# An experts' loop with a pinned order on four engines, the output product taken from two parts of both sides, and three overflow blocks moved into the loop

## The chip, the cores and the metric

The kernel runs on one core of one Trainium2 chip. Its five engines work side by side, each through its own queue of instructions in order: TensorE (PE, with its weight loads as PEld), ScalarE (ACT), VectorE (DVE), GpSimd (POOL) and SyncE (SP), which only issues DMAs here. The metric is the device time of one execution in microseconds (us), the median of three runs. Before the change it is 2878.36 us (2875.5 to 2880.1).

## The reference, cut to what matters

A trunk of two layers over 1024 tokens of 1024 features. Each layer ends in a mixture of 32 experts; every token goes to two of them. The change touches only this part:

```python
def routed_experts(ht, gate_w, expert_id, w_gate, w_up, w_down):
    ...
    def block_mlp(args):
        tok, e = args
        xb = h_pad[tok]
        hid = jax.nn.silu(xb @ w_gate[e]) * (xb @ w_up[e])
        return hid @ w_down[e]
    yb = lax.map(block_mlp, (row_tok.reshape(n_blocks, ROW_BLOCK), block_e))
    y = jax.ops.segment_sum(yb.reshape(R, D) * row_w[:, None], row_tok, num_segments=T + 1)
```

A block is 128 rows of one expert. `w_gate` and `w_up` of an expert are 1024x256 each, `w_down` is 256x1024, all float32: 3 MB for one expert.

## The kernel before, in words

The experts' stage of a layer is `moe` (L1583). Each of the 32 experts has one block of up to 128 slots, done in a loop (L1676). What does not fit goes to overflow blocks, done after the loop behind a branch on their count; with these inputs three of them run in each layer.

For one expert `e`:

- `gather` (L1594): POOL issues an indirect DMA that brings the expert's rows of the normalised input into `xg`, one of two buffers.
- `prepare` (L1606): PE turns `xg` by eight transposes into `xT_ps`; ACT copies it, rounded, to `xT_hi`, and DVE subtracts to get the rest, `xT_lo`.
- `split_half` (L1575): the gate and up weights come in two halves of 1 MB (`w_gu`, a ring of five buffers, loaded by SP). ACT casts a half to `w_hi`, DVE subtracts to get `w_lo`. There are three pairs of them.
- `up` (L1623): 24 matmuls (eight slices of the features, three products hi*hi, lo*hi and hi*lo) into `h_ps`; `hidden` (L1615) makes the activation `th` of it on ACT and DVE.
- `down` (L1645): two transposes of `th` into `hT_ps`, a copy back by DVE, then the output product `y_ps` in plain float32 with `w_d` (a ring of three buffers). DVE scales it into `yo` (one buffer), and POOL issues the indirect DMA that scatters `yo` to `yd` in HBM.

The loop's text gives `up(e)`, the splits, `gather(e + 2)`, `prepare(e + 1)`, `down(e - 1)` and the loads of later experts. The text is not the order on the engines: a scheduler with a timeline of its own decides that, by what it holds to be ready. The overflow blocks work in plain float32 throughout (`up_late`, L1638, and the same `down`).

`route_overflow` (L1490) works out the overflow blocks' tables; its instructions lie beside the first experts. After the stage, `sum_of` loads `yd` back, so the last scatter must have landed.

Of the kernel before, what the change touches and what calls it, by code (L numbers as in the profile page):

```python
# [10 lines left out]
F32 = mybir.dt.float32  # L11
F32R = mybir.dt.float32r
# [3 lines left out]
OP = mybir.AluOpType  # L16
# [4 lines left out]
T = 1024  # L21
D = 1024
NT = 8
NK = 8
# [28 lines left out]
class Trunk:  # L53
# [18 lines left out]
    GAP_A = (1.2, 0.3)  # L72

    def pool(self, **kw):
        if kw.get("space") is not DRAM:
            kw["reuse_waits"] = "tile"
        return self.tc.tile_pool(**kw)

# [1411 lines left out]
    def route_overflow(self, w, psum):  # L1490
# [20 lines left out]
        big = [w.tile([128, 1024], F32, name="ro_big", tag="ro") for _ in range(2)]  # L1511
        in1, in2 = (x[0:1, 0:480].rearrange("p (b e) -> p b e", e=32) for x in big)
# [9 lines left out]
        tmp = big[0][:, 512:1024].rearrange("p (t e) -> p t e", e=32)  # L1522
# [16 lines left out]
        o1 = big[0][:, 512:768].rearrange("p (t b) -> p t b", b=16)  # L1539
        nc.vector.tensor_tensor(o1, io[:, None, 0:16].to_broadcast([128, 16, 16]), bf.to_broadcast([128, 16, 16]), op=OP.is_equal)  # L1540
        oc = big[1][:, 512:1024].rearrange("p (t j b) -> p t j b", j=2, b=16)
# [15 lines left out]

    def more_tiles(self, wp):
        self.parts = [[wp.tile([128, 4, 512], F32R, name=f"w_{n}{i}") for n in ("lo", "hi")] for i in (2, 1, 0)][::-1]
        self.raw += [wp.tile([128, 4, 512], F32, name=f"w_gu{i}") for i in range(2, 5)]  # L1560
# [6 lines left out]
    def load_gu(self, l, i, e):  # L1567

        for half in range(2):
            self.nc.sync.dma_start(self.raw[(2 * i + half) % 5], self.expert_source(l, e, "moe_w_gu")[half])  # L1570

    def load_d(self, l, i, e):
        self.nc.sync.dma_start(self.wd[i % 3], self.expert_source(l, e, "moe_w_down"))

    def split_half(self, n, eng=None):  # L1575

        nc = self.nc
        raw = self.raw[n % 5]
        lo, hi = self.parts[n % 3]
        nc.scalar.copy(hi, raw)  # L1580
        (eng or nc.vector).tensor_tensor(lo, raw, hi.bitcast(F32), op=OP.subtract)  # L1581

    def moe(self, l, side, psum):  # L1583

        nc, tc = self.nc, self.tc
        with ExitStack() as s:
# [3 lines left out]
            for x in xg:  # L1590
                nc.gpsimd.memset(x, 0.0)
            scat = []
# [22 lines left out]
            def hidden(ph):  # L1615
                x = tx.tile([128, 512], F32, name="th", tag="mt")
                th = x[:, 0:256]
# [3 lines left out]
                return x  # L1621

            def up(e, x):  # L1623
                hi, lo = x
                ph = psum.tile([128, 512], F32, name="h_ps", tag="h", bufs=2)
                for k in range(NK):
                    wlo, whi = self.parts[(2 * e + k // 4) % 3]
# [3 lines left out]
                return hidden(ph)  # L1631

            def prepare_late(e):
                pt = transposed(e)
                nc.scalar.copy(late[e % 2], pt)
                return late[e % 2]

            def up_late(e, x):  # L1638

                ph = psum.tile([128, 512], F32, name="h_ps", tag="h", bufs=2)  # L1640
                for k in range(NK):
                    nc.tensor.matmul(ph, x[:, k, :], self.raw[(2 * e + k // 4) % 5][:, k % 4, :], start=(k == 0), stop=(k == NK - 1))
                return hidden(ph)

            def down(e, th):  # L1645
                w = self.wd[e % 3]
                pt = psum.tile([128, 2, 128], F32, name="hT_ps", tag="hT", bufs=1)
                for k in range(2):
                    nc.tensor.transpose(pt[:, k, :], th[:, 128 * k:128 * k + 128], self.ident)  # L1649
                hT = th[:, 256:512].rearrange("p (a b) -> p a b", a=2)  # L1650
                nc.vector.tensor_copy(hT, pt)  # L1651
                po = psum.tile([128, D], F32, name="y_ps", tag="y", bufs=1)
# [4 lines left out]
                yo = tx.tile([128, D], F32, name="yo", tag="x", bufs=1)  # L1657
                nc.vector.scalar_tensor_tensor(yo, po, self.wsl[:, e:e + 1], gt2, op0=OP.mult, op1=OP.mult)  # L1658
                st = nc.gpsimd.indirect_dma_start(out=self.yd, out_offset=bass.IndirectOffsetOnAxis(ap=self.idx_s[:, e:e + 1], axis=0),  # L1659
                                                  in_=yo, in_offset=None, bounds_check=2 * T - 1, oob_is_err=False)  # L1660
                for o in scat:
                    tc.declare_no_dep(st.ins, o.ins, reason="every slot holds another row")
                scat.append(st)
# [4 lines left out]
            def overflow(b):  # L1668
                eb = block_weights(b)
                self.load_gu(l, 32 + b, eb)  # L1670
                self.load_d(l, 32 + b, eb)

            gather(0)
            gather(1)
            x, prev = prepare(0), None
            for e in range(32):  # L1676
                th = up(e, x)
                for n in (2 * e + 3, 2 * e + 4):
                    if n < 64:
                        self.split_half(n)  # L1680
                if e + 1 < 32:
                    if e + 2 < 32:
                        gather(e + 2)
                    x = prepare(e + 1)
                if e == 0:
                    nc.sync.dma_start(gt2, self.mod_row(l, 5).partition_broadcast(128))
                if prev is not None:
                    down(*prev)
                prev = (e, th)
                if e < 28:  # L1690
                    self.load_gu(l, e + 4, e + 4)
                if 0 < e < 30:
                    self.load_d(l, e + 2, e + 2)
                if e == 2:
                    self.route_overflow(xp, psum)
                if e == 29:
                    self.load_gu(l, 32, block_weights(0))
            late = [xp.tile([128, 8, 128], F32, name="xT", tag="ro") for _ in range(2)]
            gather(32)
            gather(33)  # L1700
            self.load_d(l, 32, block_weights(0))
            down(*prev)
            x = prepare_late(32)

            n = nc.values_load(self.ovf[0:1, 0:1], min_val=0, max_val=15)
            with ExitStack() as ifs:
                for b in range(15):
                    ifs.enter_context(tc.If(n > b))
                    if b + 2 < 15:
                        gather(34 + b)  # L1710
                    if b + 1 < 15:
                        overflow(b + 1)
                    down(32 + b, up_late(32 + b, x))
                    if b + 1 < 15:
                        x = prepare_late(33 + b)
# [38 lines left out]
    def layer(self, l, x_src):  # L1754

        nc = self.nc
# [12 lines left out]
        def more():  # L1769

            self.wo_stack.close()
            self.more_tiles(se.enter_context(self.pool(name=f"wE{l}", bufs=1, side=here)))
            self.load_gu(l, 1, 1)
            for n in range(3):
                self.split_half(n, nc.gpsimd)
            for e in (2, 3):
                self.load_gu(l, e, e)

        with ExitStack() as s:
            psum = Banks(**{n: s.enter_context(self.pool(name=f"ps{n}e{l}", bufs=b, space=PSUM))  # L1780
                            for n, b in (("tp", 2), ("po", 4), ("pl", 2))})
            self.out_proj(l, there, psum, lambda: (self.load_gu(l, 0, 0), self.load_d(l, 0, 0)), more)
        if l == 0:
            self.dump("xm", self.xm)
        with ExitStack() as s:
            psum = s.enter_context(self.pool(name=f"psE{l}", bufs=1, space=PSUM))
            wp = s.enter_context(self.pool(name=f"wD{l}", bufs=1, side=here))
            self.wd += [wp.tile([128, 2, D], F32, name=f"w_d{i}") for i in range(1, 3)]
            for e in (1, 2):
                self.load_d(l, e, e)  # L1790
            self.moe(l, there, psum)
# [114 lines left out]
```

## Time and profile before

| what | us |
|---|---|
| median of three runs | 2878.36 |
| profiled execution | 2890.55 |
| its span, first to last instruction | 2888.7 |
| PE busy | 2452.3 (85%) |
| DVE busy | 1845.5 (64%) |
| ACT busy | 1063.5 (37%) |
| POOL busy | 721.3 (25%) |

The span is what the trace covers; the profiled execution is some 2 us longer than its span and 12 us longer than the median. The two experts' stages lie at about 1031 to 1448 us and 2424 to 2836 us of the span. Busy shares are averages over stages that have different limits, so the stage has to be read by itself.

### The profile page before, as it was taken

The numbers are of one execution on the slowest core, as the hardware profiler recorded it, in microseconds if no ns is written. First come the engines' busy times: TensorE is split into PE (matmuls) and PEld (weight loads), VectorE is DVE, ScalarE is ACT, GpSimd is POOL, SyncE is SP. The second block draws the span as 40 slices with busy tenths as digits, with TensorE's granted clock in tenths as the row PEclk, the third lists the DMA queues.
The fourth block names the chain that finished last, engine by engine and source line by source line (L and its number), as shares of the span: only waits on it lengthen the run. The fifth ranks groups of instructions, "written<-read, shape, count | busy, mean of one in ns | idle before, by whom it ended". The sixth has DMA issues, their size and how long they took to land.

```text
span 2888.7 us, 45371 instructions
## 1 busy us (share of the span) xinstructions
PE 2452.3 (85%) x17281; PEld 1842.3 (64%) x17281; DVE 1845.5 (64%) x3927; ACT 1063.5 (37%) x1908; POOL 721.3 (25%) x569
## 2 busy tenths in 40 slices
PE   5999987998789779999849888889877986999991
PEld 3766666787678656666427666778756775666650
DVE  5358785555684767767264689756467566776745
ACT  3333332343463224444133343334345331444421
POOL 4122232222420511111141222221242032111113
PEclk8989998998899779999969989899889986999996
DMA  8477575452442359899551434453443224998874
GB/s 285 157 233 215 178 239 135 134 147 93 161 127 93 140 190 328 312 329 336 188 203 52 136 122 140 151 155 115 127 158 114 98 100 147 342 350 317 306 261 186
DMA packets 264230, 548.99 MB, mean 190 GB/s; under 512 B 77048, under 2 KB 181440, under 8 KB 233280
## 3 DMA queue, kind: packets, MB, share of 16 engines
q1 hardware_dynamic: 235424, 490.90, 50.6%
q0 software_dynamic: 23952, 40.99, 3.9%
q10 hardware_dynamic: 4624, 14.06, 1.2%
q8 instruction: 141, 2.31, 0.3%
q14 instruction: 89, 0.73, 0.1%
HBM read 467.68 MB, written 120.09 MB: 203 GB/s over the span
## 4 chain that ended last, share of the span: by engine, by line
PE 52%; DVE 23%; DMA 11%; ACT 7%; issue 5%; POOL 1%; SPq 1%; DVEq 0%; ACTq 0%; POOLq 0%
PE y_ps L1655 8%; PE pj L335 5%; PE pj L336 5%; PE pj L337 5%; DVE w_lo L1581 4%; ACT w_hi L1580 4%; PE h_ps L1629 3%; PE h_ps L1628 2%; DVE sv_m L724 2%; DVE sv_t L726 2%; PE h_ps L1630 2%; PE po L1284 2%; DMA ada_w<-in_ada_w 2%; DMA yd<-yo,idx_s 2%; PE po L1285 2%
## 5 line engine op out<-in xcount | busy, mean ns | idle before, releaser
L1581 DVE TENSOR_TENSOR w_lo<-w_gu,w_hi 128x2048 fp32r<-128x2048 f32 x122 | 279.6, 2292 | 206.3 <-ACT w_hi L1580 202.1
L1580 ACT CAST w_hi<-w_gu 128x2048 fp32r<-128x2048 f32 x128 | 244.0, 1908 | 384.6 <-PE h_ps L1629 367.4
L335 PE MATMUL pj<-hh,wa_hi 128*128 128x512 f32 x800 | 341.6, 427 | 2.7 <-ACT wa_hi L322 1.9
L336 PE MATMUL pj<-hl,wa_hi 128*128 128x512 f32 x800 | 332.0, 415 | 1.1 <-DVE hl L312 1.1
L337 PE MATMUL pj<-hh,wa_lo 128*128 128x512 f32 x800 | 328.9, 413 | 3.3 <-POOL wa_lo L323 3.3
L1655 PE MATMUL y_ps<-w_d,th 128*128 128x512 f32 x560 | 260.3, 608 | 40.9 <-DVE th L1651 25.5
L1628 PE MATMUL h_ps<-w_hi,xT_hi 128*128 128x512 f32 x512 | 225.8, 441 | 3.9 <-ACT xT_hi L1611 3.9
L1629 PE MATMUL h_ps<-w_hi,xT_lo 128*128 128x512 f32 x512 | 210.8, 412 | 2.6 <-DVE xT_lo L1612 2.6
L1630 PE MATMUL h_ps<-w_lo,xT_hi 128*128 128x512 f32 x512 | 203.2, 397 | 0.0
L1655 PEld LDWEIGHTS y_ps<-w_d,th 128*128 128x128 f32 x560 | 101.3, 190 | 156.9 <-issue 103.3
L323 POOL TENSOR_TENSOR wa_lo<-wa_raw,wa_hi 128x1024 fp32r<-128x1024 f32 x50 | 122.0, 2441 | 315.6 <-ACT wa_hi L322 262.0
L335 PEld LDWEIGHTS pj<-hh,wa_hi 128*128 128x128 f32 x800 | 157.8, 197 | 42.0 <-issue 7.4
L337 PEld LDWEIGHTS pj<-hh,wa_lo 128*128 128x128 f32 x800 | 156.8, 196 | 39.5 <-POOL wa_lo L323 4.6
L336 PEld LDWEIGHTS pj<-hl,wa_hi 128*128 128x128 f32 x800 | 157.8, 197 | 37.2 <-issue 4.5
L1659 POOL DMA_INDIRECT yd<-yo,idx_s x70 | 70.5, 1008 | 402.2 <-DVE yo L1658 323.6
L1595 POOL DMA_INDIRECT xg<-h2d,idx_g x74 | 80.1, 1082 | 299.2 <-PE hT_ps L1649 250.7
L1629 PEld LDWEIGHTS h_ps<-w_hi,xT_lo 128*128 128x128 f32 x512 | 98.2, 192 | 50.5 <-DVE xT_lo L1612 30.9
L1658 DVE SCALAR_TENSOR_TENSOR yo<-y_ps,wsl,gt 128x1024 f32<-128x1024 f32 x70 | 89.5, 1279 | 52.2 <-PE y_ps L1655 27.0
L1628 PEld LDWEIGHTS h_ps<-w_hi,xT_hi 128*128 128x128 f32 x512 | 98.4, 192 | 36.7 <-issue 12.9
L724 DVE TENSOR_TENSOR sv_m<-sv_t,sv_n 64x31 f32<-64x31 f32 (+15 forms) x248 | 104.5, 421 | 23.0 <-DMA sv_n<-sp_z 18.5
L1154 ACT ACTIVATE at_p<-at_s,at_mx 128x256 f32<-128x256 f32 (+7 forms) x128 | 94.9, 742 | 63.7 <-DVE at_mx L1152 63.2
L1152 DVE TENSOR_REDUCE at_mx<-at_s 128x1 f32<-128x256 f32 (+7 forms) x128 | 95.8, 753 | 31.3 <-PE at_s L1150 30.4
(438 smaller groups left out, 5428.7 us busy)
## 6 DMA issues: line engine op xcount, KB each, us to landing
w_gu<-in_moe_w_gu SPq DMA_DIRECT2D x144, 1024.0 KB
w_d<-in_moe_w_down SPq DMA_DIRECT2D x72, 1024.0 KB
ada_w<-in_ada_w SPq DMA_DIRECT2D x80, 512.0 KB
wa_raw<-in_w_in SPq DMA_DIRECT2D x50, 512.0 KB
sp_z<-z SPq DMA_DIRECT2D x32, 768.0 KB
b_zz<-sp_z SPq DMA_DIRECT2D x32, 512.0 KB
cy<-yd SPq DMA_DIRECT2D x16, 1024.0 KB
qkv<-qst SPq DMA_DIRECT2D x48, 256.0 KB
```

The source lines that it names most:

```text
L323: nc.gpsimd.tensor_tensor(lo, raw, hi.bitcast(F32), op=OP.subtract)
L335: nc.tensor.matmul(ps, hi[:, k, :], self.hh[k][:, sl], start=(k == 0), stop=False)
L336: nc.tensor.matmul(ps, hi[:, k, :], self.hl[k][:, sl], start=False, stop=False)
L337: nc.tensor.matmul(ps, lo[:, k, :], self.hh[k][:, sl], start=False, stop=(k == NK - 1))
L724: eng.tensor_tensor(t3, tt[:, 0:j + 1, j].unsqueeze(2).to_broadcast([64, j + 1, 31 - j]), nt[:, j, j + 1:32].unsqueeze(1).to_broadcast([64 ...
L1152: nc.vector.tensor_reduce(mx, ps[:, 0:n], axis=AX.X, op=OP.max, negate=True)
L1580: nc.scalar.copy(hi, raw)
L1581: (eng or nc.vector).tensor_tensor(lo, raw, hi.bitcast(F32), op=OP.subtract)
L1628: nc.tensor.matmul(ph, hi[:, k, :], whi[:, k % 4, :], start=(k == 0), stop=False)
L1629: nc.tensor.matmul(ph, lo[:, k, :], whi[:, k % 4, :], start=False, stop=False)
L1630: nc.tensor.matmul(ph, hi[:, k, :], wlo[:, k % 4, :], start=False, stop=(k == NK - 1))
L1655: nc.tensor.matmul(po[:, 512 * half:512 * half + 512], hT[:, k, :], w[:, k, 512 * half:512 * half + 512], start=(k == 0), stop=(k == 1))
```

## The change

All of it is in the experts' stage.

- `in_order` (L81 of the changed kernel) ties every instruction of PE, ACT, DVE and POOL in the loop to the one written before it on the same engine. In the loop these four engines run in the order of the text, and the text is written anew.
- The output product is made of three products of float32r parts, as the up product was: `w_dh` (two buffers, cast by ACT) and `w_dl` (one buffer, subtracted by POOL) of the weights, and two parts of `hT`, the first copied by ACT, the second subtracted by DVE. It takes 12 matmuls in place of 4 float32 ones.
- The ring of `w_gu` has four buffers in place of five, that of `w_d` two in place of three.
- The loop runs over 35 blocks: 32 experts and three overflow blocks (`MORE_E`), whose expert is read from a register by SP. The branch after the loop starts at the fourth overflow block.
- `route_overflow` takes its work tile from another pool.

The core of the diff:

```diff
+    def split_d(self, i, part):
+        hi = self.wdh[i % 2]
+        if part == 0:
+            self.nc.scalar.copy(hi, self.wd[i % 2])
+        else:
+            self.nc.gpsimd.tensor_tensor(self.wdl, self.wd[i % 2], hi.bitcast(F32), op=OP.subtract)
...
+            def turned(e):
+
+                pt = hidden_turned(e)
+                nc.scalar.copy(hT[:, 0], pt)
+                nc.vector.tensor_tensor(hT[:, 1], pt, hT[:, 0].bitcast(F32), op=OP.subtract)
...
+            def down(e):
+                whi, wlo = self.wdh[e % 2], self.wdl
+                po = psum.tile([128, D], F32, name="y_ps", tag="y", bufs=1)
+                hi, lo = hT[:, 0], hT[:, 1]
+                for n, (x, w) in enumerate(((hi, whi), (lo, whi), (hi, wlo))):
+                    for half in range(2):
+                        cs = slice(512 * half, 512 * half + 512)
+                        for k in range(2):
+                            nc.tensor.matmul(po[:, cs], x[:, k, :], w[:, k, cs], start=(n + k == 0), stop=(n + k == 3))
+                scaled(e, po)
...
             gather(0)
             gather(1)
-            x, prev = prepare(0), None
-            for e in range(32):
...
+            x, last = prepare(0), {}
+            for e in range(N):
+                with self.in_order(last):
+                    ph = up(e, x)
+                    if e + 1 < N:
+                        self.split_half(2 * e + 3)
+                    if e:
+                        turned(e - 1)
+                    if e + 1 < N:
+                        x = prepare(e + 1)
+                    hidden(e, ph)
+                    self.split_d(e, 0)
                 if e == 0:
                     nc.sync.dma_start(gt2, self.mod_row(l, 5).partition_broadcast(128))
...
+                with self.in_order(last):
+                    if e:
+                        down(e - 1)
+                    self.split_d(e, 1)
+                    if e:
+                        scatter(e - 1)
+                    if e + 2 < N:
+                        gather(e + 2)
+                        self.split_half(2 * e + 4)
+                for n in (2 * e + 7, 2 * e + 8):
+                    if n < 2 * N:
+                        self.load_gu(l, n, expert(n // 2))
+                if e + 2 < N:
+                    self.load_d(l, e + 2, expert(e + 2))
```

What this does to the instructions on three engines, in the middle of the first layer's loop. First POOL, before the change, through two experts (`yd` is the scatter's target, `xg0` and `xg1` are the two gather buffers):

```order
L1659 DMA yd0_615<-yo_11099,idx_s_10450 2048x1024
L1595 DMA xg1_10478<-h2d0_614,idx_g_10451 128x1024
L1659 DMA yd0_615<-yo_11165,idx_s_10450 2048x1024
L1595 DMA xg0_10477<-h2d0_614,idx_g_10451 128x1024
L1659 DMA yd0_615<-yo_11231,idx_s_10450 2048x1024
```

And POOL in the changed kernel, through two experts:

```order
L1605 TENSOR_TENSOR w_dl_10468<-w_d0_9797,w_dh0_10469 128x2048
L1689 DMA yd0_615<-yo_11849,idx_s_10448 2048x1024
L1621 DMA xg0_10476<-h2d0_614,idx_g_10449 128x1024
L1605 TENSOR_TENSOR w_dl_10468<-w_d1_10467,w_dh1_10470 128x2048
L1689 DMA yd0_615<-yo_11925,idx_s_10448 2048x1024
L1621 DMA xg1_10477<-h2d0_614,idx_g_10449 128x1024
```

POOL had only DMAs to issue; now the subtraction for `w_dl` of expert e stands first, then the scatter of e - 1, then the gather of e + 2.

PE before, from the end of one expert's `up` to the start of the next one's:

```order
L1630 MATMUL h_ps<-w_lo_10322,xT_hi 128x512
L1603 MATMUL xT_ps<-ident,xg_10477 128x128 x8
L1649 MATMUL hT_ps<-ident,th 128x128 x2
L1655 MATMUL y_ps<-w_d_10469,th 128x512 x4
L1628 MATMUL h_ps<-w_hi_10327,xT_hi 128x512
```

And PE in the changed kernel, at the same place:

```order
L1655 MATMUL h_ps<-w_lo_10325,xT_hi 128x512
L1673 MATMUL hT_ps<-ident,th 128x128 x2
L1629 MATMUL xT_ps<-ident,xg_10477 128x128 x8
L1703 MATMUL y_ps<-w_dh_10470,hT 128x512 x8
L1703 MATMUL y_ps<-w_dl,hT 128x512 x4
L1653 MATMUL h_ps<-w_hi_10326,xT_hi 128x512
```

The transposes of `th` now stand ahead of those of `xg`, and the 12 matmuls of the output product take the place of the 4.

ACT in the changed kernel, through one expert:

```order
L1679 CAST hT<-hT_ps 128x256
L1637 CAST xT_hi<-xT_ps 128x1024
L1643 ACTIVATE th<-h_ps 128x256
L1603 CAST w_dh_10470<-w_d_10467 128x2048
L1594 CAST w_hi_10322<-w_gu_10328 128x2048
L1594 CAST w_hi_10324<-w_gu_10329 128x2048
```

The cast for `w_dh` of expert e stands behind the copy of `xT_hi` for e + 1 and behind the activation of e; before, neither it nor the copy of `hT` was on this engine.

## Rows read from the trace of the kernel before

**Rows 1.** Windows: stretch, length; busy PE, PEld, DVE, ACT, POOL; clock, DMA share, GB/s.

```profile
1100.00:1200.00 100.00, 94.40 (x381) 63.52 (x380) 71.18 (x63) 45.37 (x37) 18.69 (x18) 1.00 0.89 318
1031.00:1039.80 8.80, 7.95 (x25) 6.44 (x26) 1.99 (x4) 1.01 (x1) 0.99 (x1) 0.50 0.10 26
1394.10:1397.50 3.40, 0.04 (x1) 0.00 (x0) 1.56 (x2) 0.00 (x0) 0.00 (x0) 1.00 1.00 410
1398.30:1401.70 3.40, 3.40 (x6) 1.33 (x5) 0.00 (x0) 0.00 (x0) 0.20 (x1) 0.50 0.99 366
```

**Rows 2.** Timeline of one expert in the first layer's loop: start, duration.

```profile
1145.62 1.03 PE L1603 MATMUL xT_ps<-ident,xg 128*128 128x128 f32 x8
...
1146.93 1.07 POOL L1595 DMA_INDIRECT xg<-h2d,idx_g  x1 [3.90 <-PE hT_ps L1649]
...
1154.87 0.39 PE L1629 MATMUL h_ps<-w_hi,xT_lo 128*128 128x512 f32 x1
...
1155.10 0.39 PE L1630 MATMUL h_ps<-w_lo,xT_hi 128*128 128x512 f32 x1
...
1156.69 1.03 PE L1603 MATMUL xT_ps<-ident,xg 128*128 128x128 f32 x8
```

**Rows 3.** Timeline, first layer, ahead of the loop: POOL and DVE at once.

```profile
983.25 13.43 POOL L1581 TENSOR_TENSOR w_lo<-w_gu,w_hi 128x2048 fp32r<-128x2048 f32 x3 [8.43 <-ACT w_hi L1580]
...
983.48 13.87 DVE L1476 TENSOR_SCALAR r_ohr<-r_io,r_rk 128x128 f32<-128x128 f32 x6
997.55 0.71 DVE L1476 TENSOR_SCALAR r_ohr<-r_io,r_rk 128x128 f32<-128x128 f32 x2 [0.20 <-PE r_pv L1477]
```

**Rows 4.** Instructions by line, 1100 to 1300 us: busy, mean ns, idle before.

```profile
L1581 DVE TENSOR_TENSOR w_lo<-w_gu,w_hi 128x2048 fp32r<-128x2048 f32 x37 | 84.8, 2293 | 59.5 <-ACT w_hi L1580 58.0
L1580 ACT CAST w_hi<-w_gu 128x2048 fp32r<-128x2048 f32 x37 | 70.6, 1908 | 114.8 <-PE h_ps L1629 114.8
...
L1618 ACT ACTIVATE th<-h_ps 128x256 f32<-128x256 f32 x18 | 6.8, 376 | 0.0
```

**Rows 5.** Timeline at the start of the first layer's loop.

```profile
1031.17 1.95 PE L1603 MATMUL xT_ps<-ident,xg 128*128 128x128 f32 x8
...
1033.15 1.01 ACT L1611 CAST xT_hi<-xT_ps 128x1024 fp32r<-128x1024 f32 x1 [18.67 <-PE xT_ps L1603]
...
1042.91 1.03 PE L1603 MATMUL xT_ps<-ident,xg 128*128 128x128 f32 x8
```

**Rows 6.** Timeline, overflow blocks: a scatter, a gather, the loads beside them.

```profile
1417.58 0.99 POOL L1659 DMA_INDIRECT yd<-yo,idx_s  x1 [9.67 <-DVE yo L1658]
1418.88 1.03 POOL L1595 DMA_INDIRECT xg<-h2d,idx_g  x1 [0.31 <-issue]
...
1419.97 0.33 SPq L1573 DMA_DIRECT2D w_d<-in_moe_w_down  x1
```

**Rows 7.** DMA queues, 1422.7 to 1424.3 us: packets, MB, share of 16 engines.

```profile
q0 software_dynamic: 144, 0.00, 5.1%
```

**Rows 8.** Timeline, second layer: a gather with no load beside it.

```profile
2426.27 0.99 POOL L1595 DMA_INDIRECT xg<-h2d,idx_g  x1 [5.58 <-PE ro_pv L1549]
```

**Rows 9.** DMA queues, 2427.9 to 2430.2 us, behind that gather.

```profile
q0 software_dynamic: 144, 0.52, 79.8%
```

**Rows 10.** Timeline, overflow blocks: a scatter and the DVE instruction awaiting its landing.

```profile
1385.75 1.01 POOL L1659 DMA_INDIRECT yd<-yo,idx_s  x1 [5.35 <-DVE yo L1658]
...
1395.94 1.28 DVE L1658 SCALAR_TENSOR_TENSOR yo<-y_ps,wsl,gt 128x1024 f32<-128x1024 f32 x1 [5.09 <-DMA yd<-yo,idx_s]
```

**Rows 11.** Timeline: the first layer's last scatter, its landing; the second layer's ends.

```profile
1443.51 1.00 POOL L1659 DMA_INDIRECT yd<-yo,idx_s  x1 [10.63 <-DVEq L1706]
...
1448.41 0.94 POOL L718 MEMSET sv_t<- 64x1024 f32 x1 [3.90 <-DMA yd<-yo,idx_s]
...
2424.05 1.95 PE L1603 MATMUL xT_ps<-ident,xg 128*128 128x128 f32 x8
...
2836.45 4.45 SPq L1721 DMA_DIRECT2D cy<-yd  x8
```

More of the change, by code (lines that the diff above doesn't have):

```diff
@@ L77, in pool, with in_order @@
         return self.tc.tile_pool(**kw)
+    @contextmanager
+    def in_order(self, last):
+        engines = [e.engine for e in (self.nc.tensor, self.nc.scalar, self.nc.vector, self.nc.gpsimd)]
+        traced = self.nc.cur_bb.bb.instructions
+        n = len(traced)
+        yield
+        for i in traced[n:]:
+            if i.engine in engines:
+                if i.engine in last:
+                    self.tc.add_manual_dep(i, last[i.engine].name, mybir.DependencyInfo(mybir.DependencyClass.NoSync, mybir.DependencyReason.DATA),
+                                           reason="program order")
+                last[i.engine] = i
     def rsqrt(self, pool, x, n, eps, scale, name):
@@ L1630, in up @@
                     nc.tensor.matmul(ph, hi[:, k, :], wlo[:, k % 4, :], start=False, stop=(k == NK - 1))
-                return hidden(ph)
+                return ph
             def prepare_late(e):
                 pt = transposed(e)
-                nc.scalar.copy(late[e % 2], pt)
-                return late[e % 2]
+                nc.scalar.copy(late, pt)
+                return late
             def up_late(e, x):
@@ L1641, in up_late, with hidden_turned @@
                 for k in range(NK):
[L1642 to L1646, printed above, removed]
+                    nc.tensor.matmul(ph, x[:, k, :], self.raw[(2 * e + k // 4) % self.RAW][:, k % 4, :], start=(k == 0), stop=(k == NK - 1))
+                hidden(e, ph)
+            def hidden_turned(e):
                 pt = psum.tile([128, 2, 128], F32, name="hT_ps", tag="hT", bufs=1)
@@ new lines, in moe, with scaled, scatter @@
+            yos = {}
+            def scaled(e, po):
+                yo = yos[e] = tx.tile([128, D], F32, name="yo", tag="x", bufs=1)
+                nc.vector.scalar_tensor_tensor(yo, po, self.wsl[:, e:e + 1], gt2, op0=OP.mult, op1=OP.mult)
+            def scatter(e):
+                st = nc.gpsimd.indirect_dma_start(out=self.yd, out_offset=bass.IndirectOffsetOnAxis(ap=self.idx_s[:, e:e + 1], axis=0),
+                                                  in_=yos.pop(e), in_offset=None, bounds_check=2 * T - 1, oob_is_err=False)
+                for o in scat:
+                    tc.declare_no_dep(st.ins, o.ins, reason="every slot holds another row")
+                scat.append(st)
@@ L1656, in down @@
                                          start=(k == 0), stop=(k == 1))
[L1657 to L1663, printed above, removed]
+                scaled(e, po)
+                scatter(e)
             def block_weights(b):
@@ L1669, in overflow, with expert @@
                 eb = block_weights(b)
-                self.load_gu(l, 32 + b, eb)
+                for half in range(2):
+                    self.load_gu(l, 64 + 2 * b + half, eb)
                 self.load_d(l, 32 + b, eb)
+            N = 32 + self.MORE_E
+            def expert(e):
+                return e if e < 32 else block_weights(e - 32)
             gather(0)
             gather(1)
-            x, prev = prepare(0), None
-            for e in range(32):
[L1677 to L1684, printed above, removed]
+            x, last = prepare(0), {}
@@ L1685, in moe @@
+            for e in range(N):
[7 more added lines that the diff above has]
+                        x = prepare(e + 1)
+                    hidden(e, ph)
+                    self.split_d(e, 0)
                 if e == 0:
                     nc.sync.dma_start(gt2, self.mod_row(l, 5).partition_broadcast(128))
[L1687 to L1688 removed]
@@ L1700, in moe @@
[L1700 to L1703, printed above, removed]
+            turned(N - 1)
+            down(N - 1)
+            scatter(N - 1)
+            late = self.lay.tile([128, 8, 128], F32, name="xT", tag="sg")
             n = nc.values_load(self.ovf[0:1, 0:1], min_val=0, max_val=15)
             with ExitStack() as ifs:
-                for b in range(15):
+                for b in range(self.MORE_E, 15):
                     ifs.enter_context(tc.If(n > b))
-                    if b + 2 < 15:
-                        gather(34 + b)
+                    if b == self.MORE_E:
+                        gather(32 + b)
+                        overflow(b)
+                    x = prepare_late(32 + b)
@@ L1787, in layer @@
             wp = s.enter_context(self.pool(name=f"wD{l}", bufs=1, side=here))
-            self.wd += [wp.tile([128, 2, D], F32, name=f"w_d{i}") for i in range(1, 3)]
-            for e in (1, 2):
-                self.load_d(l, e, e)
+            self.wd += [wp.tile([128, 2, D], F32, name="w_d1")]
+            self.wdl = wp.tile([128, 2, D], F32R, name="w_dl")
+            self.wdh = [wp.tile([128, 2, D], F32R, name=f"w_dh{i}") for i in range(2)]
+            self.load_d(l, 1, 1)
             self.moe(l, there, psum)
```

78 lines of the change are left out of this document (38 added, 40 removed).

## The prediction

> **What bounds the kernel now.** I read the windows first, since the change lies in the experts' two stages alone. In the middle of the first layer's loop PE is busy 94.40 of 100 us at full clock, and the DMA engines are 0.89 busy [rows 1]: PE bounds the loop, the loads stand just behind. The timeline gives the pace: from the transposes of one expert's rows to those of the next it is 1156.69 - 1145.62 = 11.07 us [rows 2]. What matters for the change is where the gather stands. It is issued at 1146.93, right behind the transposes that free its buffer [rows 2], and this buffer is read again two experts later, at about 1145.6 + 22.1 = 1167.8: the gather has some 21 us, so nobody waits for it. No row of the loop shows PE waiting for `xg`.
>
> A stage runs from the first transposes to the landing of the last scatter: 1448.41 - 1031.17 = 417.2 us in the first layer and 2836.45 - 2424.05 = 412.4 in the second [rows 5, 11], 829.6 together.
>
> **The change part by part.**
>
> *The output product on PE.* Matmuls of parts start 0.23 us apart (1155.10 - 1154.87) [rows 2]. So `up` is 24 x 0.23 = 5.5 us, the new output product 12 x 0.23 = 2.8, and the ten transposes some 1.3: 9.6 us of PE for one block, under the 11.07 of now. This would be the pace if nothing else were late.
>
> *POOL.* `w_dl` is new: 2048 columns a row, as `w_lo` on POOL ahead of the loop, 13.43 / 3 = 4.5 us each [rows 3]. In the pinned order it stands ahead of the scatter of e - 1 and of the gather of e + 2. A scatter takes 1.0 us and a gather 1.0 to issue, with 0.3 between them [rows 6].
>
> *The gather's lead.* The gather of e + 2 is now read in iteration e + 1, straight behind `up(e + 1)`. But it stands behind `w_dl(e)`, and that one waits for two things of iteration e: its cast `w_dh(e)` on ACT, the last of three instructions behind the transposes of e + 1, and the one `w_dl` buffer, free when `down(e - 1)` ends, behind the same transposes on PE. So from the transposes of one block to those of the next there is a closed chain. I add it up with T = start of the transposes of e + 1.
>
> - PE's clock. PE will idle some microseconds in each turn. In the tail it was idle for 3.4 us (0.04 busy), and then its clock was at 0.50 (1.2 GHz) for 3.4 us [rows 1]; at the start of the loop it was at 0.50 for 8.8 us behind thin work [rows 1]. I take half clock for the first 5 us, nearer to the tail's.
> - The transposes then take 1.95 us, and ACT's copy starts 2.0 us behind their start [rows 5].
> - `down(e - 1)` follows them on PE. From T + 2 to T + 5 some 6.6 of its matmuls pass at 0.46 us, the other 5.4 in 1.2 us at 0.23: it ends at T + 6.2.
> - ACT meanwhile does `xT_hi` 1.0, `th` 0.38, `w_dh` 1.9 [rows 4, 5], with 0.3 of gaps: done at T + 5.6. PE is later; POOL starts `w_dl` at T + 6.2 and ends it at T + 10.7.
> - Scatter 0.3 + 1.0, then 0.3: the gather is issued at T + 12.3.
> - From issue to use. With a scatter 1.3 us ahead and a load 1.1 us behind, a gather issued at 1418.88 had its 144 packets moved only between 1422.7 and 1424.3 [rows 6, 7], 3.8 to 5.4 us behind. This is the neighbourhood that the new loop has: DVE's `w_lo` works in SBUF alone, and such instructions look to be held by POOL's: six of them took 13.87 us beside POOL's 13.43, two more of the same right behind 0.71 [rows 3]. So `w_lo(2e + 4)` runs from T + 10.7 to T + 13.0, and the load into the buffer that it frees goes out 0.7 us behind the gather. I take 5.4 and 0.2 for the semaphore: 5.6.
>
> The pace is 12.3 + 5.6 = **17.9 us** for one block. The ends: alone a gather issued at 2426.27 had moved 0.52 MB by 2430.2, 3.9 us [rows 8, 9]; a scatter whose landing DVE awaited, under a DMA share of 1.00, took 10.2 us (1385.75 to 1395.94) [rows 1, 10]. I keep 3.9 and, for the upper end, 8, halfway from 5.6 to 10.2, since in the new loop the loads have landed before the next gather goes out: 3 MB in 17.9 us, where now they take 0.89 of 11.07. With PE at full clock throughout, ACT sets the start of `w_dl` at T + 4.6, and with 3.9 the pace is 14.6.
>
> The Trainium skill (DMA: Bandwidth & Descriptors, Anatomy of one DMA) gives such a DMA from POOL 2.0 us plus its bytes at 436 GB/s. For 64 rows of 4 KB this would be an estimate of 2.6 us, a pace of 14.9 and a total of some 3118 us. The gather of rows 6 and 7 moved next to nothing and still took over 3.8 us, so the trace does not agree beside loads, and I go by the rows.
>
> *What is hidden.* The shorter product, the copy of `hT` now on ACT, the ring of four for `w_gu` and of two for `w_d`, and the seven small products of the overflow tables that now stand together ahead of one block's transposes all lie in the time that PE waits for the gather: I cost them at nothing. Were the gather early, ACT's 1.9 us more and the smaller rings would still have 9.6 us of PE as cover.
>
> *The overflow blocks.* Three more turns of the loop at 17.9 us take the place of three float32 blocks behind it; both are in the stage sums. The branch behind the loop finds nothing left to do.
>
> *The sum.* First to second transposes as now, 1042.91 - 1031.17 = 11.7 [rows 5]. To the third 15: no scatter stands there yet and the clock is up. Then 32 turns at 17.9 = 573. From the last transposes: `down(32)`, `up(34)` and the transposes of `th` to T + 12, `down(33)` to T + 15; `w_dl(34)` on POOL to T + 20, ahead of scatter 33, which lands 4.9 us behind its issue (1443.51 to 1448.41) [rows 11] and frees `yo` at T + 25; the last scale 1.3, the last scatter and its landing: T + 31.5. Together 11.7 + 15 + 573 + 31.5 = 631 us for a stage, 1262 for both, against 829.6: 432 us more. On the profiled execution's 2890.6 this is 3323; the median is 12 us under that one, so **3310 us**. One microsecond of pace is 64 us of time.
>
> **The rivals.**
>
> 1. *The same chain, but short.* The loads are over when the gather goes out, it lands in 3.9 us, and PE's clock stays up: 14.6 us a turn, 3310 - 64 x 3.3 = 3099. Up to 15.5 I count to this case (3156). For it: the lone gather of rows 8. Against: the loads are released by the same `w_dl`. The skill's rule above would lead here.
> 2. *The same chain, but long.* The gather queues among 3 MB of loads that go out within 3 us of it, as the scatter of rows 10 did: 8 us or more, 20.3 a turn, 3464 and up. For it: three loads come together now. Against: in rows 10 the engines were full for long before.
> 3. *The gather is in time.* Then PE sets the pace at 9.6 to 9.8 us, a stage is 11.7 + 33 x 9.8 + 24 = 359, and the time is 2878 - (829.6 - 718) = 2767, faster than before. This turns on POOL: chain and pace meet when `w_dl` and the landing together take under 4 us or so, against 4.5 + 3.9 at the least by rows 3 and 9. Only a POOL subtraction far faster than those ahead of the loop would do.
> 4. *Nothing comes of it.* A pace of 11.2 would leave the time as it is; it needs the same two to take 6 us together.
>
> **How the numbers follow.** Forecast, pace 15.5 to 20: 0.73. Rival 1: 0.13. Rival 2: 0.09. Rival 3: 0.04. Rival 4: 0.01. The predicted time is that of the forecast, 3310. The range leaves out the ends of rivals 1 and 2 and all of 3 and 4: 3150 (pace 15.4) to 3450 (pace 20.1). Within 0.2% of 2878 us, about 6 us, a measurement of this kernel could not tell the two apart. Faster 0.04, same 0.01, slower 0.95.
>
> **What would show it.** In the profile of the changed kernel, transposes of `xg` some 18 us apart, PE idle 5 to 7 us ahead of each and released by the gather's DMA; POOL in the order `w_dl`, scatter, gather with 4.5, 1.0 and 1.0 us and `w_dl` released by PE's `y_ps` or ACT's `w_dh`; PE's clock at 0.50 for part of every turn; DMA share near 0.55; DVE's `w_lo` stretched beside `w_dl`. The prediction is wrong if the transposes wait for anything else, if a turn is under 12 us, or if `w_dl` takes well under 4 us.

## The result and the profile after

The changed kernel takes 3763.16 us (median of four runs, 3757.24 to 3768.12) against 2878.59 for the kernel before beside it: a ratio of 1.307, 95% interval 1.305 to 1.310. The forecast was 3310, in a range from 3150 to 3450. The direction and the chain were right; a turn, from the transposes of one block's rows to those of the next, is 25 us long where 17.9 was forecast.

First the page of the changed kernel, its engines and the costliest groups (busy, mean ns | idle before, releaser):

```profile
PE 2514.3 (67%) x17593; PEld 2018.2 (54%) x17593; DVE 2111.5 (56%) x3945; ACT 1235.3 (33%) x2058; POOL 1216.5 (32%) x635
...
L1629 PE MATMUL xT_ps<-ident,xg 128*128 128x128 f32 x560 | 134.0, 419 | 844.8 <-DMA xg<-h2d,idx_g 844.8
L1605 POOL TENSOR_TENSOR w_dl<-w_d,w_dh 128x2048 fp32r<-128x2048 f32 x70 | 323.2, 4617 | 1022.8 <-PE y_ps L1703 906.8
...
L1595 DVE TENSOR_TENSOR w_lo<-w_gu,w_hi 128x2048 fp32r<-128x2048 f32 x134 | 514.5, 3878 | 20.1 <-ACT w_hi L1594 19.5
...
L1689 POOL DMA_INDIRECT yd<-yo,idx_s x70 | 190.4, 2720 | 20.9 <-issue 15.9
...
L1621 POOL DMA_INDIRECT xg<-h2d,idx_g x70 | 131.6, 1880 | 35.0 <-issue 20.3
```

PE's busy time grew by 62 us alone, from 2452.3. What grew is one wait: PE waits 844.8 us for the gather, where the kernel before had no such wait in its loop, and the median is up by 884.6 us. The second stage runs from 2863.25 to 3714.51, 851.3 us against 412.4 [rows 11]. `w_lo` takes 3.88 us in the mean where it took 2.29 [rows 4], and the two indirect DMAs take POOL 2.7 and 1.9 us where they took 1.0 [rows 2, 6].

One turn, from the timeline of the changed kernel (rows left out: those of `up`, PE's weight loads, the smaller instructions of ACT and DVE):

```profile
1311.19 1.94 PE L1629 MATMUL xT_ps<-ident,xg 128*128 128x128 f32 x8 [13.99 <-DMA xg<-h2d,idx_g]
...
1314.36 1.90 ACT L1603 CAST w_dh<-w_d 128x2048 fp32r<-128x2048 f32 x1
...
1316.35 1.42 PE L1703 MATMUL y_ps<-w_dl,hT 128*128 128x512 f32 x4
...
1318.01 4.62 POOL L1605 TENSOR_TENSOR w_dl<-w_d,w_dh 128x2048 fp32r<-128x2048 f32 x1 [16.37 <-PE y_ps L1703]
1319.00 7.98 DVE L1595 TENSOR_TENSOR w_lo<-w_gu,w_hi 128x2048 fp32r<-128x2048 f32 x2
1322.79 2.88 POOL L1689 DMA_INDIRECT yd<-yo,idx_s  x1 [0.17 <-issue]
...
1324.81 0.33 SPq L1586 DMA_DIRECT2D w_gu<-in_moe_w_gu  x1
1325.22 0.38 SPq L1589 DMA_DIRECT2D w_d<-in_moe_w_down  x1
1325.98 1.88 POOL L1621 DMA_INDIRECT xg<-h2d,idx_g  x1 [0.31 <-issue]
...
1327.01 0.33 SPq L1586 DMA_DIRECT2D w_gu<-in_moe_w_gu  x1
...
1336.84 1.51 PE L1629 MATMUL xT_ps<-ident,xg 128*128 128x128 f32 x6 [13.38 <-DMA xg<-h2d,idx_g]
```

This is the forecast chain, link by link: transposes, `down`, `w_dl`, scatter, gather, landing. The lengths differ: `w_dl` starts at T + 6.8 (T is the start of the transposes), the gather goes out at T + 14.8, and from its issue to PE 10.9 us pass. Three loads of 1 MB go out between 1.2 us before the gather and 1.0 us behind it. Two of them fill `w_gu` buffers that the two `w_lo` subtractions free, the second behind its end at 1326.98; the third, `w_d`, is freed by `w_dl`. The windows of the same turn (columns as in [rows 1]):

```profile
1311.19:1318.00 6.81, 6.80 (x22) 5.77 (x23) 2.17 (x4) 4.83 (x4) 0.00 (x0) 0.57 0.00 0
1318.00:1322.80 4.80, 4.80 (x22) 3.96 (x22) 4.80 (x2) 1.97 (x2) 4.63 (x2) 1.00 0.00 0
1322.80:1326.00 3.20, 0.66 (x4) 0.29 (x3) 3.20 (x2) 0.37 (x1) 2.89 (x2) 1.00 0.24 33
1326.00:1329.00 3.00, 0.00 (x0) 0.00 (x0) 1.31 (x2) 0.00 (x0) 1.85 (x1) 0.71 0.81 322
1329.00:1332.40 3.40, 0.00 (x0) 0.00 (x0) 0.00 (x0) 0.00 (x0) 0.00 (x0) 0.50 1.02 412
1332.40:1336.50 4.10, 0.00 (x0) 0.00 (x0) 0.00 (x0) 0.00 (x0) 0.00 (x0) 0.50 0.54 219
```

For 11.6 us no byte moves; then the loads and the gather share the DMA engines, at a share of 1.02 for 3.4 us, while PE, DVE, ACT and POOL are all idle. Which queue is served shows in the DMA queues of two stretches, 1322.8 to 1329.3 (first row) and 1329.3 to 1336.8 (the other two): packets, MB, share of 16 engines.

```profile
q1 hardware_dynamic: 161, 1.19, 54.7%
...
q1 hardware_dynamic: 271, 1.96, 62.0%
q0 software_dynamic: 288, 0.23, 9.0%
```

POOL's queue (q0) moves nothing in the first stretch. The 288 packets of the scatter and the gather, 0.23 MB, all come in the second, though POOL was done with the scatter at 1325.67. There the two queues pass nearly packet for packet, 288 against 271, and POOL's two transfers are through only when 1.96 MB of loads have passed beside them.

The changed kernel tells in its own turns what the loads cost. The trace has the landing of 68 of its 70 gathers. The six with at most one load issued within 3 us of them, at the beginning and the end of each stage, land 3.8 to 4.5 us behind their issue; the 62 with two to six such loads land after 9.9 to 11.6 us.

### The profile page after: what moved, and what is told of

It is laid out like the page before. It is cut to its first block, busy times and chain, and to the rows that moved or that the text cites. A ratio compares the mean times of both kernels' runs of the same rounds, so it can differ in the third digit from the quotient of the medians.

```text
span 3766.3 us, 46325 instructions
## 1 busy us (share of the span) xinstructions
PE 2514.3 (67%) x17593; PEld 2018.2 (54%) x17593; DVE 2111.5 (56%) x3945; ACT 1235.3 (33%) x2058; POOL 1216.5 (32%) x635
## 5 line engine op out<-in xcount | busy, mean ns | idle before, releaser
L1629 PE MATMUL xT_ps<-ident,xg 128*128 128x128 f32 x560 | 134.0, 419 | 844.8 <-DMA xg<-h2d,idx_g 844.8
L1605 POOL TENSOR_TENSOR w_dl<-w_d,w_dh 128x2048 fp32r<-128x2048 f32 x70 | 323.2, 4617 | 1022.8 <-PE y_ps L1703 906.8
L1629 PEld LDWEIGHTS xT_ps<-ident,xg 128*128 128x128 f32 x560 | 108.5, 221 | 858.4 <-issue 856.4
L1638 DVE TENSOR_TENSOR xT_lo<-xT_ps,xT_hi 128x1024 fp32r<-128x1024 f32 x70 | 85.7, 1225 | 792.9 <-ACT xT_hi L1637 792.9
L1595 DVE TENSOR_TENSOR w_lo<-w_gu,w_hi 128x2048 fp32r<-128x2048 f32 x134 | 514.5, 3878 | 20.1 <-ACT w_hi L1594 19.5
L1637 ACT CAST xT_hi<-xT_ps 128x1024 fp32r<-128x1024 f32 x70 | 70.9, 1013 | 1007.6 <-PE xT_ps L1629 1007.6
L1703 PE MATMUL y_ps<-w_dh,hT 128*128 128x512 f32 x560 | 224.8, 566 | 3.4 <-DVE yo L1686 2.5
L1689 POOL DMA_INDIRECT yd<-yo,idx_s x70 | 190.4, 2720 | 20.9 <-issue 15.9
L1703 PEld LDWEIGHTS y_ps<-w_dh,hT 128*128 128x128 f32 x560 | 157.2, 295 | 39.1 <-ACTq L1773 2.9
L1603 ACT CAST w_dh<-w_d 128x2048 fp32r<-128x2048 f32 x70 | 133.5, 1908 | 0.0
```

Of the source, the lines that this page charges most:

```text
L1595: eng.tensor_tensor(lo, raw, hi.bitcast(F32), op=OP.subtract)
L1605: self.nc.gpsimd.tensor_tensor(self.wdl, self.wd[i % 2], hi.bitcast(F32), op=OP.subtract)
L1629: nc.tensor.transpose(pt[:, k, :], x[:, 128 * k:128 * k + 128], self.ident)
L1703: nc.tensor.matmul(po[:, cs], x[:, k, :], w[:, k, cs], start=(n + k == 0), stop=(n + k == 3))
```

## The experiments

Three theories went in. **A**: the gather's place on POOL closes the turn, and it lands late because it goes out among the loads. **B**: POOL's `w_dl` and DVE's `w_lo` hold each other, and that sets the turn. **C**: PE's half clock does. "Turn" is the median of the 34 distances between transposes, in the first and in the second layer; the changed kernel has 25.2 and 24.9 us, 25.0 together. All but the last two runs are single executions, beside a kernel before of 2877.76 us (the first four) or 2882.77 (the next four).

**The gather at the head of the iteration.**

```diff
                 with self.in_order(last):
+                    if e + 2 < N:
+                        gather(e + 2)
                     ph = up(e, x)
...
                         scatter(e - 1)
                     if e + 2 < N:
-                        gather(e + 2)
                         self.split_half(2 * e + 4)
```

> The gather of e + 2 is issued at the start of iteration e, ahead of w_dl(e); nothing else is moved. Theory A (the turn is closed by the gather's place on POOL, behind w_dl and the scatter, and the gather lands late, 11 us behind its issue, among the 3 MB of loads that the same w_dl releases): PE no longer waits for xg, and the turn falls from 26 us to about 15, where the scatter, still behind w_dl, has to land before yo is written again (4.7 for w_dl, up to 10 for the landing). About 2990 us, 2900 to 3100. Rival B (w_dl on POOL and w_lo on DVE hold each other, and their sum with the rest sets the turn): the gather's place changes little, the turn stays over 22 us, over 3500 us. Rival C (PE's half clock sets it): the turn falls by no more than the 3 us that the clock costs in a turn, about 3560 us.

Measured 2943.98 us, a turn of 12.7 and 12.5. Moving one instruction takes 12.4 of the 14 us by which a turn had grown over the 11.07 before. PE's wait for the gather does not vanish, but between 1150 and 1350 us it falls from 13.6 us a turn to 1.6. What limits it now is the next closed chain, in its timeline:

```profile
1199.63 1.28 DVE L1686 SCALAR_TENSOR_TENSOR yo<-y_ps,wsl,gt 128x1024 f32<-128x1024 f32 x1 [4.55 <-DMA yd<-yo,idx_s]
...
1201.20 2.80 POOL L1689 DMA_INDIRECT yd<-yo,idx_s  x1 [1.01 <-DVE yo L1686]
...
1212.34 1.28 DVE L1686 SCALAR_TENSOR_TENSOR yo<-y_ps,wsl,gt 128x1024 f32<-128x1024 f32 x1 [4.78 <-DMA yd<-yo,idx_s]
```

There is one `yo`: the next scale waits until the scatter has landed, 11.1 us behind its issue, and that is 12.7 us from scale to scale.

**The gather ahead of the scatter, both still behind `w_dl`.**

```diff
                     self.split_d(e, 1)
+                    if e + 2 < N:
+                        gather(e + 2)
                     if e:
                         scatter(e - 1)
                     if e + 2 < N:
-                        gather(e + 2)
                         self.split_half(2 * e + 4)
```

> On POOL the gather of e + 2 is put between w_dl(e) and the scatter of e - 1; nothing else. Theory A: the gather goes out 3.2 us earlier in each turn (the scatter's 2.9 us of issue and 0.3 between), its landing is the same 11 us: a turn of 23 us, about 3550 us. If the loads, still released at the same moment, hold it to the same landing in absolute time, the turn stays nearer to 26, 3700 us. Rivals B and C: no change, 3763 us.

Measured 3544.95 us, a turn of 21.6 and 21.5: 3.5 us shorter, about the 2.88 + 0.31 of the scatter. The scatter is on the chain, as A has it.

**No loads from the fifth iteration on.** The loads of the later experts' weights are left out; these experts are computed with the weights that lie there.

```diff
-                    if n < 2 * N:
+                    if n < 2 * N and e < 4:
...
-                if e + 2 < N:
+                if e + 2 < N and e < 4:
                     self.load_d(l, e + 2, expert(e + 2))
```

> Left out: the loads of the experts' weights issued from iteration 4 of the loop on (w_gu and w_d), so the later blocks work with old weights; the order on the four engines is the same. Theory A: the gather has the DMA engines for itself and lands 4 to 5 us behind its issue in place of 11; a turn of about 20 us, about 3370 us. Rival B: the landing and the turn stay as they are if the wait comes from POOL and DVE alone, 3763 us. If the late landing comes from POOL's writing of the descriptors beside DVE's w_lo, it stays at 9 us or more, over 3620 us.

Measured 3427.46 us, a turn of 18.9 and 19.1. From its timeline, and the window from the first transposes shown to the start of `w_dl`:

```profile
1299.06 1.90 POOL L1621 DMA_INDIRECT xg<-h2d,idx_g  x1 [0.30 <-issue]
...
1303.31 1.94 PE L1629 MATMUL xT_ps<-ident,xg 128*128 128x128 f32 x8 [6.74 <-DMA xg<-h2d,idx_g]
...
1308.69 4.63 POOL L1605 TENSOR_TENSOR w_dl<-w_d,w_dh 128x2048 fp32r<-128x2048 f32 x1 [7.74 <-PE y_ps L1703]
...
1316.67 1.88 POOL L1621 DMA_INDIRECT xg<-h2d,idx_g  x1 [0.31 <-issue]
...
1321.69 1.94 PE L1629 MATMUL xT_ps<-ident,xg 128*128 128x128 f32 x8 [7.52 <-DMA xg<-h2d,idx_g]
```

```profile
1303.31:1308.69 5.38, 5.38 (x22) 4.72 (x23) 2.11 (x4) 3.40 (x4) 0.00 (x0) 0.73 0.00 0
```

From issue to use it is 4.25 and 5.0 us in place of 10.9. The loads cost 6 us of every turn, but not by the landing alone. The turn shown takes 18.4 us against the 25.65 above: 5.8 of the difference are the landing, and 1.4 come from `w_dl`, which starts at T + 5.4 in place of T + 6.8. PE had been idle for 6.7 us ahead of T and not 14.0, and its clock up to `w_dl` is 0.73 and not 0.57.

**`w_dl` on DVE, the order as it was.**

```diff
-            self.nc.gpsimd.tensor_tensor(self.wdl, self.wd[i % 2], hi.bitcast(F32), op=OP.subtract)
+            self.nc.vector.tensor_tensor(self.wdl, self.wd[i % 2], hi.bitcast(F32), op=OP.subtract)
```

> The subtraction for w_dl is done by DVE at its place in the text (behind yo, ahead of w_lo); POOL issues only scatter and gather, in this order, the gather still directly ahead of its use. Theory A: the scatter waits for yo at 8 us of the turn, the gather goes out at 9.3 us ahead of the loads, lands in 4 to 5 us: a turn of 13.5 to 14.5 us, about 2970 us. Rival B: with nothing on POOL to hold DVE, the turn is DVE's sum, 10.6 us, about 2740 us.

Measured 3425.53 us, a turn of 20.2: a miss of 455 us. With `w_dl` gone from POOL the gather was to be early enough. Its timeline:

```profile
1305.45 2.28 DVE L1605 TENSOR_TENSOR w_dl<-w_d,w_dh 128x2048 fp32r<-128x2048 f32 x1
1305.82 2.80 POOL L1689 DMA_INDIRECT yd<-yo,idx_s  x1 [15.38 <-DVE yo L1686]
...
1307.76 0.33 SPq L1589 DMA_DIRECT2D w_d<-in_moe_w_down  x1
1308.92 1.91 POOL L1621 DMA_INDIRECT xg<-h2d,idx_g  x1 [0.30 <-issue]
...
1309.96 2.53 SPq L1586 DMA_DIRECT2D w_gu<-in_moe_w_gu  x2
...
1317.93 1.94 PE L1629 MATMUL xT_ps<-ident,xg 128*128 128x128 f32 x8 [8.03 <-DMA xg<-h2d,idx_g]
```

The loads moved forward with the subtraction that frees their buffers, so the gather is among them here too, 9.0 us from issue to use. What I had missed is that the subtraction releases both: the load of `w_d` goes out at its end, 1307.73, and POOL's issue of the scatter, ahead of the gather, lasts until 0.9 us behind it.

**Gather first, and the scatter ahead of `w_dl`.** It comes on top of the first experiment's edit and was to take `w_dl` off the `yo` chain. In the rows of that experiment `w_dl` is not on it: POOL waits for `yo` there, 1.01 us.

```diff
                     if e:
                         down(e - 1)
-                    self.split_d(e, 1)
                     if e:
                         scatter(e - 1)
+                    self.split_d(e, 1)
```

> As with the gather at the start of iteration e, and the scatter of e - 1 also ahead of w_dl(e) on POOL, behind yo only. Theory A: the scatter's landing, for which yo waited some 4.5 us a turn with the gather alone moved, leaves the chain by the 4.6 us of w_dl; what is left is w_dl beside DVE's w_lo, which hold each other: DVE's own 8.3 us and 4.5 of POOL's, at most 12.8 us, at least the landing's 11.5. About 2890 us, 2840 to 2945. If the landing slips as the loads come with it, no gain over the 2944 us of the gather alone.

Measured 3126.08 us, a turn of 14.6 in both layers: 236 us over the forecast and worse than the gather's move alone. Its timeline shows theory B at work:

```profile
1207.98 4.59 POOL L1605 TENSOR_TENSOR w_dl<-w_d,w_dh 128x2048 fp32r<-128x2048 f32 x1
1208.92 5.80 DVE L1595 TENSOR_TENSOR w_lo<-w_gu,w_hi 128x2048 fp32r<-128x2048 f32 x1 [1.86 <-ACT w_hi L1594]
...
1212.73 2.88 POOL L1621 DMA_INDIRECT xg<-h2d,idx_g  x1 [0.17 <-issue]
...
1214.65 0.41 DVE L1680 TENSOR_TENSOR hT<-hT_ps,hT 128x256 fp32r<-128x256 f32 x1
...
1215.11 1.75 PE L1703 MATMUL y_ps<-w_dh,hT 128*128 128x512 f32 x4 [3.20 <-DVE hT L1680]
```

`w_lo` begins beside `w_dl`, ends 2.15 us after it, and DVE's small `hT` subtraction stands behind `w_lo`. The second of PE's three products waits for it, 3.2 us. In the first experiment `w_dl` ran from 1208.04 to 1212.65 us, while DVE waited 4.78 us for the scatter.

**The same with `w_dl` on DVE** (the last two edits together).

> Gather first, scatter behind yo, and the subtraction for w_dl on DVE behind the scatter's yo; POOL issues DMAs alone. Theory A: DVE's sum is 10.6 us; the scatter's landing, beside the loads, 10 to 11.5: a turn of 10.8 to 11.5 us, about 2830 us, 2800 to 2870. Rival B, that the hold between POOL and DVE is the main cost, also puts it there, but then the kernel with the scatter early and w_dl on POOL has to be over 100 us slower than this one; by theory A it is some 60.

Measured 2886.28 us, 16 over the range, a turn of 11.7 and 11.0, 240 us less than the run above, where B asked for over 100. So B is a real second cost, about 3.4 us a turn once the gather is out of the way. It is not what closed the turn of the changed kernel, since with `w_dl` still on POOL the gather's move opened it. It may lengthen that chain too: with `w_dl` on DVE and the gather where it was, the turn was 4.8 us shorter. How much of this is the hold and how much the length of `w_dl` on POOL, no run separates.

**The plain product in the new order.** The float32 product of the kernel before with its rings of five and three, in the pinned order with the overflow blocks in the loop, `hT` copied whole by ACT, gather first, scatter behind `yo`. The second run gives `yo` a second buffer. The split product with a second `yo` was not tried.

```diff
-                yo = yos[e] = tx.tile([128, D], F32, name="yo", tag="x", bufs=1)
+                yo = yos[e] = (xp.tile([128, D], F32, name="yo", tag="yo", bufs=1) if e % 2 else tx.tile([128, D], F32, name="yo", tag="x", bufs=1))
```

> The pinned order and the three overflow blocks in the loop are kept, the output product is the plain float32 one of the kernel before (no w_dh, no w_dl, ring of five for w_gu and of three for w_d), hT is copied by ACT, the gather stands first and the scatter behind yo. Theory A: the pinned order as such costs nothing, what cost was the gather's place behind w_dl; PE then sets the turn with 5.5 + 1.3 + 3.4 us and little else: 10.3 to 10.6 us against 11.07 before, about 2810 us, 2785 to 2840. If a pinned order is itself slower than the scheduler's, over 2880 us.

> As the plain product in the pinned order, with a second buffer for yo, so that no scale waits for the scatter of the block before. If the scatter's landing (7 to 10 us behind its issue beside loads) still holds yo at a turn of 10.4 us, this one is 10 to 40 us faster than the one with a single yo; if not, the same within 6 us.

Measured 2884.37 us with one `yo` and 2816.07 with two, turns of 11.2 and 10.2 over both layers. The first is over the 2880 us named for a slow pinned order; the second shows that the order is not what held it. With one buffer, the groups by line from 1150 to 1350 us:

```profile
L1685 DVE SCALAR_TENSOR_TENSOR yo<-y_ps,wsl,gt 128x1024 f32<-128x1024 f32 x18 | 23.1, 1284 | 60.5 <-DMA yd<-yo,idx_s 57.5 <-PE h_ps L1654 2.9
```

The single `yo` is the limit again. That the plain and the split product with one `yo` take the same time (2884 and 2886) need not have one cause: between 1150 and 1350 us DVE waits 20.4 us for the scatter in the split one, and PE 27.5 us for `hT`. The two-buffer kernel was timed again in five rounds, and without the overflow blocks in the loop (`MORE_E = 0`) in three:

> The same kernel as e7y_plain_two_yo, timed in five rounds: pinned order and overflow in the loop, plain product, gather at the head of the iteration, scatter behind yo, two yo buffers. Theory A (the turn of the changed kernel was closed by the gather's place, and the order and the overflow in the loop are worth something by themselves): about 2816 us, ratio to the kernel before 0.975 to 0.982. Rival (the one look was a chance of that chip): ratio 0.99 to 1.01.

> e7y_plain_two_yo with the three overflow blocks taken out of the loop again, so all overflow blocks stand behind it as in the kernel before. If the overflow in the loop is what gains: three blocks a layer, two layers, go from some 10.1 us in the loop to some 13 to 16 us behind it, so 2835 to 2865 us. If the pinned order or the plain gather place alone gains and the overflow blocks cost the same on either side: 2816 us.

The first is 2812.43 us, a ratio of 0.975 to the kernel before (95% interval 0.9735 to 0.9771): faster than the kernel before and than the changed one. The second is 2861.26, ratio 0.993 (0.991 to 0.995). The groups and the window of the first one's loop:

```profile
L1685 DVE SCALAR_TENSOR_TENSOR yo<-y_ps,wsl,gt 128x1024 f32<-128x1024 f32 x19 | 24.4, 1284 | 7.3 <-PE y_ps L1700 7.3
```

```profile
1150.00:1350.00 200.00, 195.23 (x820) 137.00 (x819) 149.49 (x115) 104.00 (x98) 113.76 (x40) 1.00 0.96 351
```

No wait for the scatter is left, PE is busy 195 of 200 us, and the DMA share is 0.96.

The two differ by 49 us, but this is not what the overflow blocks in the loop gain over the kernel before. That one issued the first overflow gathers and loads ahead of its branch. The branch of the changed kernel issues them behind the loop (the first gather at 1361.89 us, after the last expert's scatter), and with `MORE_E = 0` this comes into every layer: the turns into its three overflow blocks take 26.2, 18.6 and 15.3 us. Three points of the first layer tell the parts apart: the first transposes, those of the 32nd expert, and the instruction that follows the last landing. For the kernel before, the middle one ([rows 5, 11] have the others):

```profile
1378.02 1.03 PE L1603 MATMUL xT_ps<-ident,xg 128*128 128x128 f32 x8
```

With the overflow blocks in the loop:

```profile
1025.30 1.94 PE L1629 MATMUL xT_ps<-ident,xg 128*128 128x128 f32 x8 [5.34 <-DMA xg<-h2d,idx_g]
...
1348.22 1.07 PE L1629 MATMUL xT_ps<-ident,xg 128*128 128x128 f32 x8
...
1403.91 0.94 POOL L733 MEMSET sv_t<- 64x1024 f32 x1 [3.54 <-DMA yd<-yo,idx_s]
```

And behind it:

```profile
1017.47 1.94 PE L1629 MATMUL xT_ps<-ident,xg 128*128 128x128 f32 x8 [5.55 <-DMA xg<-h2d,idx_g]
...
1339.52 1.03 PE L1629 MATMUL xT_ps<-ident,xg 128*128 128x128 f32 x8
...
1422.55 0.94 POOL L733 MEMSET sv_t<- 64x1024 f32 x1 [3.22 <-DMA xg<-h2d,idx_g]
```

Up to the 32nd expert it is 346.9 us before, 322.9 and 322.1 in these two; from there on 70.4, 55.7 and 83.0. The second layer has 347.1, 320.6 and 319.2, then 65.3, 56.3 and 81.4. So over both layers of these profiled executions the order, the gather's place, `hT` on ACT and the second `yo` are worth some 50 us together (no run separates them all), and the overflow blocks in the loop some 24; the late branch costs 29.

## Why the prediction was right in kind and wrong in size

- **The chain** was right. Every link came in the forecast order, with the forecast releasers: `w_dl` by PE's `y_ps`, the transposes by the gather's DMA. Moving the gather opens it.
- **`w_dl` at T + 6.2, 4.5 long**: 6.8 and 4.62 measured. PE's granted clock was 0.57 in the mean of these 6.8 us; half clock for the first 5 was near it.
- **The failed step is "From issue to use ... 5.6"**, together with the reason given for its upper end, "since in the new loop the loads have landed before the next gather goes out". The loads of the turn before had landed: the share was 0.00 for 11.6 us. But the loads of this turn go out with the gather: the subtractions that free their buffers, `w_dl` and the two `w_lo`, are those that POOL's scatter and gather wait for too. Of the three loads only one had been counted, 0.7 us behind the gather. Measured: 10.9 us in the turn shown, +5.3 on a turn. The row that told it was at hand: the scatter of [rows 10] took 10.2 us beside full DMA engines, and I halved the way to it in favour of the tail's gather [rows 6, 7], which had one load beside it. Without the loads the measured 4.25 to 5.0 lies between the lone gather's 3.9 [rows 8, 9] and the forecast's 5.6, and the turn of 18.9 to 19.1 is near the forecast.
- **"Scatter 0.3 + 1.0, then 0.3"** was a second, smaller error: 0.16 + 2.88 + 0.31, 1.75 us more. The prices came from the overflow blocks, where DVE had no `w_lo` to do. The gather's own issue is 0.85 longer for the same reason, inside the 10.9.
- The sum with these numbers: 0.6 + 0.1 + 1.75 + 5.3 = 7.75 us more than 17.9 in this turn, which is 25.65 long; with the median, 25.0, it is 7.1 x 64 = 454 us on the 3310, so 3764 against 3763. The form of the sum held; that it meets to 1 us is luck, since single turns off the median cancel: the second of the first layer took 19.8 us where 15 was taken, its last two 19.0 and 17.9.
- **Rival 2**, the long chain, is what happened: it was given 0.09 with "three loads come together now" as its reason. Its condition, three loads or more that go out within 3 us of the gather, holds in all turns of the loop but the first and the last few. The weight against it, that in [rows 10] the engines were full for long before, misled: here no byte had moved for 11.6 us, and the gather was late all the same.
- **The Trainium skill's** 2.0 us plus bytes (DMA: Bandwidth & Descriptors, Anatomy of one DMA) did not hold beside loads, 10.9 us. Without loads 4.25 and 5.0 us pass for less than 0.25 MB; of these 1.9 are POOL's issue beside `w_lo`, and the 2.4 and 3.1 left are near the skill's figure.
- **What was costed at nothing**: ACT's new casts, the smaller rings and the overflow tables stayed hidden behind PE's wait: through the first layer's loop PE waits 418.8 us for the gather and no engine for a load of weights, and the tables' products are done before the gather beside them lands. **The overflow blocks** did take turns of the loop: 70 gathers in all.
- **Rival 4's condition** was added up wrong: with the chain's terms at full clock, T + 4.6 and 1.6, a pace of 11.2 needs `w_dl` and the landing to take 5 us together, not 6. Nothing hangs on it.
- Theory C was not tried by itself. Were PE at full clock throughout, `w_dl` could start when `w_dh` is done, at 1316.26 in place of 1318.01, and the transposes ahead of ACT's work would take 1.03 us [rows 2] in place of 1.94: some 2.7 us a turn, by estimate. The run without loads got back 1.4 of it.

## What to carry to other kernels

When an order is pinned, look for the closed chain: an in-order queue in which a prefetch stands behind work that needs the result of the step before turns the prefetch into a part of the turn, and one moved line gave 12 of 14 us back. A DMA's landing time is to be taken from a row with the loads in flight that the new place will have; ask what else the releasing instruction sets free, since the loads come with it. Once the first chain is open, look at once for the next one: here a single output buffer behind a scatter of 11 us.

## What the hardware showed that I had not expected

**POOL's issue of an indirect DMA waits for DVE's subtraction.** From the changed kernel, a scatter in the loop and the layer's last but one, for which no `w_lo` is left:

```profile
1422.59 2.89 POOL L1689 DMA_INDIRECT yd<-yo,idx_s  x1 [0.15 <-issue]
...
1872.64 0.99 POOL L1689 DMA_INDIRECT yd<-yo,idx_s  x1 [0.17 <-issue]
```

Of the changed kernel's 140 scatters and gathers 130 begin beside a `w_lo`, and all of these end 0.87 to 0.90 us behind its end. The same in single rows: in the run with `w_dl` on DVE it ends at 1307.73 and the scatter at 1308.62; in the turn of the changed kernel shown above `w_lo` ends at 1326.98 and the gather at 1327.86; in the run with the scatter early `w_lo` ends at 1214.72 and the gather at 1215.61. It reads as if the writing of about 0.9 us starts only when DVE is done. In the kernel before the gather began at 1146.93, 0.17 us ahead of the end of a `w_lo`, and ended 0.90 behind it [rows 2]: the same, with little to wait for. The Trainium skill (SBUF — State Buffer, SBUF: two separate sides) tells of a port pair that DVE and GpSimd share and by which DVE can keep GpSimd from writing descriptors; it names DVE's copies in a two-port mode, and for instructions with two SBUF inputs only a GpSimd instruction that reads SBUF. The rows here show it for subtractions with two SBUF inputs, beside a POOL that issues a DMA.

**POOL's DMA queue is served late beside loads.** With no loads, the queue of the run without them moved 144 packets between 1299.06 and 1301 us, behind a scatter that POOL finished at 1298.75:

```profile
q0 software_dynamic: 144, 0.25, 33.0%
```

In the changed kernel nothing of q0 moved for 3.6 us after POOL had finished the scatter, while q1 did. The Trainium skill (DMA: Bandwidth & Descriptors, Queues, rings and completion order) says that an engine takes turns between the queues that it has work for; by that alone the scatter's packets should have come among those of the first load. From 1329.3 us on the trace agrees: the queues pass 288 and 271 packets side by side. Whether POOL's packets waited in their queue before that, or their descriptors came late, no row here tells.
